# A hybrid DeltaNet and attention layer: later preparation steps, a gate by tanh, and one turn of the value blocks

## The chip, the cores and the metric

The kernel runs on one core of a Trainium2 chip. The metric is the device time of one execution in microseconds (us). The engines are TensorE (PE in the profile, its weight loads PEld), VectorE (DVE), ScalarE (ACT), GpSimd (POOL) and SyncE (SP), which issues most transfers. Each engine works through its own queue of instructions in order.

## The reference

One layer over 1024 latent tokens and 256 context tokens of width 1024. Cut to what matters here:

```python
px = modulate(rms_norm(x, norm1_w), sh1, sc1) @ w_in        # latent; pc the same for the context
qkv = short_conv(p[..., :3 * DN_WIDTH], conv_w)             # depthwise, 5 taps, then SiLU
a_mat = eye(CHUNK) + where(strict, (kb @ k^T) * decay, 0)   # CHUNK = 64, per head and direction
u = triangular_solve(a_mat, v * beta); w = triangular_solve(a_mat, kb * exp(gam))
# scan over chunks, forward and backward, the context first; then
o = rms_norm(o, out_norm_w) * silu(z)                       # gated DeltaNet, 4 heads of 128
na = neighborhood_attention(q, k, v, k_ctx, v_ctx, rpb)     # 8 heads of 64, window 8 x 16 + all context keys
x = x + g1 * (concatenate([o, na]) @ w_out)
x = x + g2 * swiglu(modulate(rms_norm(x, norm2_w), sh2, sc2), w_ffn_in, w_ffn_out)
```

## The kernel before

Every large product is made in fp32 precision out of three products of a high and a low part (`hh`, `hl` of the normed input, `whi`, `wlo` of the weights). Weights arrive as `wraw`; ScalarE casts the high part (L198, for wide jobs `zw` L584), and POOL subtracts to get the low part (L199, L585). For wide jobs `wraw` has one buffer, so the second half of a weight block is loaded when POOL has read the first.

The input projection is a list of jobs: a `Block` gives one head's 128 columns of k, q, v (DeltaNet) or nk, nq (attention) for all 1280 tokens, `Wide` jobs give 256 columns in tiles of 128 tokens (nv the attention's values, z the gate). Their order is k0 to k3, z1, nk0 to nk2, nv0, nk3, q0 to q3, nq0 to nq3, v0, nv1, v1, v2, v3, z0. A block's result lies in PSUM banks "blk" (four); ScalarE copies them to `cr` (L452) and so frees them; then come the convolution on VectorE (L456, L460), SiLU on ScalarE (L467), and transposes in `finish`.

Beside the jobs run background generators, a few steps for each group of products:

- `block_inverses` makes the 32 x 32 inverses that the scans need: tables of decay, a substitution on VectorE (L880, L882), then 32 transposes of `N` into `U` on TensorE (L892), four to a bank "m" (two banks), which ScalarE copies out (L894). The results go to `x_d`.
- `preps` makes, in ten steps of one pair of chunks each (forward and backward), the inverse y of a chunk's matrix: `rg` on POOL (L952), a product of `rg` and a constant (L964) for the decay `e`, a product `fx` by `kk` (L984) which ScalarE copies back to `kk` (L987), and then three blocks of y of 32, 64 and 96 columns (L995), each of which needs the copy of the one before (L997 on VectorE, L998 on ScalarE). The banks are "pr" (two). y is stored to `y_d` by SP (L1007). At most two steps are alive at once.

After v3 the job z0 runs beside the first tiles of the neighbourhood attention (scores L302, softmax L304 to L308, products with the values L323); then come the scans, the output projection and the feed-forward.

A scheduler puts each engine's instructions in order from the order in which they are written and from their estimated readiness; what it decides stands fast when the program is built. `keep_in_program_order` ties one instruction to its written place.

Of the kernel before, what the change touches and what calls it, by code (L numbers as in the profile page):

```python
# [9 lines left out]
F32 = mybir.dt.float32  # L10
# [3 lines left out]
AF = mybir.ActivationFunctionType  # L14
OP = mybir.AluOpType
# [73 lines left out]
def hybrid(ctx, tc, a, dbg):  # L89
# [56 lines left out]
    nv_d = dram.tile([T, 512], F32, name="nv_d", tag="nv_d")  # L146
    nq_d = dram.tile([NAH, 2, ND, L], F16, name="nq_d", tag="nq_d")
    nk_d = dram.tile([2, NAH, ND, T], F16, name="nk_d", tag="nk_d")
    vw_d = dram.tile([128, 4, 4, 4, 128], F32, name="vw_d", tag="vw_d")
    y_d = dram.tile([2, NCH, 128, 4, 128], F32, name="y_d", tag="y_d")  # L150
    at_d = dram.tile([2, 8, 128, 4, 128], F32, name="at_d", tag="at_d")
    x_d = dram.tile([128, 2, 2, NU, 32], F32, name="x_d", tag="x_d")
# [100 lines left out]
    def attention(nw):  # L253
# [20 lines left out]

        def values(hp, half, cb):
            vw = nw.tile([128, 3, 128], F32, name="vw", tag="vw", bufs=3)
            sp.dma_start(vw, vw_d[:, hp, cb, half:half + 3])
            return vw

        def context(hp):  # L280
# [93 lines left out]
    with ExitStack() as bs:  # L374
# [188 lines left out]
        class Wide:  # L563
# [32 lines left out]
            def tiles(self):  # L596
                half = self.half
                if self.kind == "nv":
                    for t in range(NCH):
                        p = self.wide(t, 0, 256)  # L600
                        vt = cp.tile([128, 272], F32, name="zt", tag="zt", bufs=2)
                        act.copy(vt[:, :256], p[:, :256])
                        act.dma_start(nv_d[t * 128:(t + 1) * 128, half * 256:half * 256 + 256], vt[:, :256])
                        yield
                    return
                if half == 1:
                    p = bank("blk")
                    for k in range(KT):
                        for j, (ww, x) in enumerate(((self.hi, hh), (self.hi, hl), (self.lo, hh))):
                            pe.matmul(p[:16, :CT], ww[:, k, 256:272], x[k][:, :CT], start=k == 0 and j == 0,  # L610
                                      stop=k == KT - 1 and j == 2)
                    abT = cp.tile([16, 272], F32, name="abT", tag="zt", bufs=2)
                    act.copy(abT[:, :CT], p[:16, :CT])
                    yield
                for t in range(2, NCH):
                    p = self.wide(t, 0, self.n)
                    if half == 0:
                        if t % 4 == 2:
                            zg = cp.tile([128, NCH, 128], F32, name="zg", tag="kx", bufs=3)
                            zg = zg.rearrange("p a b -> p (a b)")[:, :1024]  # L620
                        act.copy(zg[:, (t - 2) % 4 * 256:(t - 2) % 4 * 256 + 256], p[:, :256])
                        if t % 4 == 1:
                            act.activation(zg, zg, AF.Silu)
                            act.dma_start(z_d[(t - 5) * 128:(t - 1) * 128, 0:256].rearrange("(c p) d -> p c d", p=128),
                                          zg.rearrange("p (c d) -> p c d", d=256))
                        yield
                        continue
                    if t == 3:
                        q = bank()
                        for i in range(2):  # L630
                            pe.transpose(q[:, i * 16:i * 16 + 16], abT[:, i * 128:i * 128 + 128], ident[:16, :16])
                        act.copy(ab[:, 0:2].rearrange("p c d -> p (c d)"), q[:, :32])
                    zt = cp.tile([128, 272], F32, name="zt", tag="zt", bufs=2)
                    act.activation(zt[:, :256], p[:, :256], AF.Silu)
                    act.copy(ab[:, t], p[:, 256:272])
                    act.dma_start(z_d[(t - 2) * 128:(t - 1) * 128, 256:512], zt[:, :256])
                    yield
# [182 lines left out]
        def block_inverses():  # L820
            with ExitStack() as gs:
# [61 lines left out]
                    yield  # L883
                flat = N.rearrange("p b r c -> p b (r c)")
                dve.memset(flat[:P, :, 0:1024:33], 1.0)
                for _ in range(4):
                    yield
                U = WK.rearrange("p d u i -> p (d u) i")
                for i0 in range(0, 32, 4):
                    p = bank()  # L890
                    for i in range(4):
                        pe.transpose(p[:, i * P:(i + 1) * P], N[:P, :, :, i0 + i].rearrange("p b r -> p (b r)"),  # L892
                                     ident[:P, :P])
                    act.copy(U[:, :, i0:i0 + 4], p[:, :4 * P].rearrange("p (i u) -> p u i", i=4))  # L894
                    if i0 % 8 == 4:
                        yield
# [15 lines left out]
        def preps():  # L912

            first_half.close()
            with ExitStack() as gs:
# [28 lines left out]
                def prep(i, got):  # L944
# [10 lines left out]
                        for q in q32:  # L955
                            act.copy(fxs[d][q, :, q], xc[q, 1])
                    yield 1
                    if i == 0:
                        yield 1
                    es = []  # L960
                    for d, c, kk, xc, at in got:
                        p = bank("pr")
                        for j in range(2):
                            pe.matmul(p, mr[:, d], fl(rgs[2 * d + j]), start=j == 0, stop=False)  # L964
                        pe.matmul(p, mr[:, 4], mneg[:, d].rearrange("p (o i) -> p o i", o=1).to_broadcast(
                            [128, 4, 128]), start=False, stop=True)
                        e = work("e", 2)
# [18 lines left out]
                    for (d, c, kk, xc, at), p in zip(got, ps):  # L986
                        act.copy(fl(kk), p)  # L987
                    yield 1
                    for n in range(1, 4):
                        blk = (q32[3 - n], q32[n])  # L990
                        cols = (slice(128 - 32 * n, 128), slice(0, 32 * n))
# [8 lines left out]
                    for d, c, kk, xc, at in got:  # L1000
                        stores.append((y_d[d, c], y[d], tick[0] + 1))

                stores, tick = [], [0]

                def flush(n):
                    while stores and stores[0][2] <= n:
# [4 lines left out]
                while live or todo or landing:  # L1011
                    if not landing and todo and (todo[0] < 2 or all(x in done for x in queries)):
                        landing.append(fetch(todo.pop(0)))
                    if landing and (not live or len(live) < 2 and live[0][1] >= 4):
                        live.append([prep(*landing.pop(0)), 0])
                    if not live:
                        yield
                    for g in list(live):
# [30 lines left out]
        for n in range(2, len(jobs) + 2):  # L1049
# [21 lines left out]
            if isinstance(j, Wide):  # L1071
                for t, _ in enumerate(j.tiles()):
                    if t > 1 or not final:
                        next(fin, 0)
                    if final and t > 2:
                        next(fill)
                    if t == 4 and nrm:
# [16 lines left out]
            for _ in fin:  # L1094
                pass
            done.add(n - 2)
            if isinstance(j, Wide) and j.kind == "nv":
                hv = slice(2 * j.half, 2 * j.half + 2)
                vlat = nv_d[CT:].rearrange("(r c) d -> r c d", c=64)
                for cb in range(4):  # L1100
                    for ch in range(4):
                        for r in range(4):
                            rows = vlat[4 * ch + r, BLKS[cb]:BLKS[cb] + 32].rearrange("c (h d) -> c h d", d=128)
                            sp.dma_start(vw_d[r * 32:r * 32 + 32, hv, cb, ch], rows[:, hv])
            if nrm:
                nrm.norm()
            if isinstance(j, Block):
# [27 lines left out]
        dve.scalar_tensor_tensor(lo, p, onw, hi.bitcast(F32), op0=OP.mult, op1=OP.subtract)  # L1135

    with ExitStack() as gs:
        sl = pools(gs, "sl", "right", 3)
        shift(gs, "spad", "right", 16)
        sw = pools(gs, "sw", "right", 2)  # L1140
        gs.callback(scan_psum.close)
        ps = psum[-1]

# [12 lines left out]
        def load(d, c, near):  # L1156

            def tile_of(name, src):
                t = work(name, 3) if name == "v" else sl.tile([128, 4, 128], F32, name=name, tag=name)
                sp.dma_start(fl(t), src)  # L1160
                return t

# [189 lines left out]
    class Stream:  # L1352
# [67 lines left out]
        def next(self, n=2):  # L1420

            while len(self.got) < n:
                self.make()
            out = [self.got.pop(0) for _ in range(n)]
            return out
# [347 lines left out]
```

## Time and profile before

| | |
|---|---|
| time, median of 3 runs | 1541.6 us (1541.44 to 1543.45) |
| the profiled execution's own time | 1541.49 us |
| its span | 1539.4 us |
| TensorE busy | 1474.1 us, 96% |
| VectorE, ScalarE, POOL busy | 993.6, 728.2, 234.8 us |
| mean granted TensorE clock | 0.988 |
| moved by DMA | 267.36 MB, mean 174 GB/s |

The span is the time from the first instruction to the last; the execution's own time has some 2 us around it. Times in timeline rows are from the span's start: a row gives the start, the busy time, engine, line, operation, output<-input, how many instructions are grouped, and in brackets the idle time of the engine in front of them with what ended it. The granted clock is a share of full speed. "SPq" rows are the issuing of transfers by SP.

### The profile page before, as it was taken

The page shows a single profiled execution, that of the slowest core. Times are in us where ns is not written, and L with a number is a line of the kernel's source. Part 1 is how long each engine was busy: PE and PEld are TensorE (multiplying, and loading weights), DVE is VectorE, ACT ScalarE, POOL GpSimd, SP SyncE. Part 2 cuts the span into 40 slices and gives each one's busy share as a digit, 9 for nine tenths or more (in the row PEclk, how much of TensorE's full clock was granted, in tenths as well). Part 3 has the DMA queues.
Part 4 walks back from the last instruction along what each step waited for, and adds up shares of the span by engine and source line. Part 5 has one row for each costly group of instructions (what it writes and reads, how often), then busy time and mean ns, then how long its engine had stood idle before and what let it go on. Part 6 is the DMA issues. An engine that isn't in the chain of part 4 may idle for free. (4 is left out here: it accounts for less than half of the span.)

```text
span 1539.4 us, 24029 instructions
## 1 busy us (share of the span) xinstructions
PE 1474.1 (96%) x8702; PEld 1231.0 (80%) x8702; DVE 993.6 (65%) x1712; ACT 728.2 (47%) x1405; POOL 234.8 (15%) x286
## 2 busy tenths in 40 slices
PE   6999998899899898999999999999999999999999
PEld 3788797777688787788888878888888888888887
DVE  4774587974464354677977379855555566599652
ACT  5442552646764236666873176333333334354440
POOL 1054500634554100111210000000000000000000
PEclk9999999999999999999999999999999999999999
DMA  9274232687655557898638503533333334798742
GB/s 387 68 212 139 60 86 79 202 239 246 182 172 170 147 142 247 278 292 253 209 90 282 183 34 109 186 106 106 107 105 103 104 102 148 248 376 275 247 143 82
DMA packets 205142, 267.36 MB, mean 174 GB/s; under 512 B 17760, under 2 KB 115552, under 8 KB 204000
## 3 DMA queue, kind: packets, MB, share of 16 engines
q1 hardware_dynamic: 194320, 258.45, 52.4%
q10 hardware_dynamic: 10704, 7.38, 1.5%
q8 instruction: 68, 1.11, 0.3%
q14 instruction: 50, 0.41, 0.1%
HBM read 201.02 MB, written 68.94 MB: 175 GB/s over the span
## 5 line engine op out<-in xcount | busy, mean ns | idle before, releaser
L404 PE MATMUL blk<-hh,whi 128*128 128x512 f32 (+1 forms) x410 | 123.0, 394 | 6.8 <-ACT cr L452 5.3
L1410 ACT CAST uhi<-ws 128x512 fp32r<-128x512 f32 x91 | 54.0, 621 | 146.0 <-PE ps L1349 96.1
L1410 ACT CAST uhi<-wq 128x512 fp32r<-128x512 f32 x101 | 61.0, 622 | 130.9 <-issue 84.6
L404 PE MATMUL blk<-hl,whi 128*128 128x512 f32 (+1 forms) x410 | 115.4, 375 | 0.3 <-DVE hl L704 0.3
L404 PE MATMUL blk<-hh,wlo 128*128 128x512 f32 (+1 forms) x410 | 114.6, 375 | 0.6 <-POOL wlo L199 0.6
L592 PE MATMUL blk<-zw,hh 128*128 128x256 f32 (+1 forms) x576 | 113.5, 291 | 1.1 <-ACT cr L452 1.0
L1411 DVE TENSOR_TENSOR ulo<-wq,uhi 128x512 fp32r<-128x512 f32 x101 | 67.5, 687 | 58.4 <-ACT uhi L1410 32.4
L1349 PE MATMUL ps<-hT,uhi 128*128 128x512 f32 x336 | 103.6, 390 | 0.0
L1349 PE MATMUL ps<-lT,uhi 128*128 128x512 f32 x336 | 103.5, 389 | 0.0
L1349 PE MATMUL ps<-hT,ulo 128*128 128x512 f32 x336 | 103.4, 389 | 0.0
L592 PEld LDWEIGHTS blk<-zw,hh 128*128 128x128 f32 x576 | 91.7, 191 | 4.0 <-ACT cr L452 1.5
L1349 PE MATMUL ps<-hB,uhi 128*128 128x512 f32 x288 | 89.2, 391 | 0.6 <-ACT hB L1524 0.6
L1349 PE MATMUL ps<-lB,uhi 128*128 128x512 f32 x288 | 88.8, 389 | 0.4 <-DVE lB L1525 0.4
L1349 PE MATMUL ps<-hB,ulo 128*128 128x512 f32 x288 | 88.6, 389 | 0.0
L404 PEld LDWEIGHTS blk<-hh,whi 128*128 128x128 f32 x410 | 69.0, 194 | 21.9 <-ACT cr L452 6.1
L404 PEld LDWEIGHTS blk<-hl,whi 128*128 128x128 f32 x410 | 72.5, 192 | 14.9 <-DVE hl L704 0.8
L404 PEld LDWEIGHTS blk<-hh,wlo 128*128 128x128 f32 x410 | 72.5, 192 | 14.9 <-POOL wlo L199 0.9
L592 PE MATMUL blk<-zw,hl 128*128 128x256 f32 (+1 forms) x288 | 82.4, 286 | 0.0
L199 POOL TENSOR_TENSOR wlo<-wraw,whi 128x1024 fp32r<-128x1024 f32 x18 | 46.6, 2586 | 194.1 <-ACT whi L198 193.9
L1349 PEld LDWEIGHTS ps<-lT,uhi 128*128 128x128 f32 x336 | 63.1, 188 | 13.2
L1349 PEld LDWEIGHTS ps<-hT,ulo 128*128 128x128 f32 x336 | 63.1, 188 | 13.2
L1349 PEld LDWEIGHTS ps<-hT,uhi 128*128 128x128 f32 x336 | 62.9, 188 | 12.9
(362 smaller groups left out, 3526.1 us busy)
## 6 DMA issues: line engine op xcount, KB each, us to landing
wq<-w_fo SPq DMA_DIRECT2D x99, 256.0 KB, 4.1
wq<-w_gu SPq DMA_DIRECT2D x88, 256.0 KB, 2.9
wad<-wa SPq DMA_DIRECT2D x64, 256.0 KB, 4.2
bt<-rpb SPq DMA_DIRECT2D x64, 192.0 KB, 3.7
t_d<-g SPq DMA_DIRECT2D x22, 512.0 KB, 3.7
fr<-t_d SPq DMA_DIRECT2D x44, 256.0 KB, 5.2
f_d<-g SPq DMA_DIRECT2D x33, 256.0 KB, 2.1
fr<-f_d SPq DMA_DIRECT2D x33, 256.0 KB, 4.2
```

The source lines that it names most:

```text
L199: lo_engine.tensor_tensor(o, r, h.bitcast(F32), OP.subtract)
L404: pe.matmul(o, ww[:, k], xx[k][:, s], start=k == 0 and j == 0, stop=k == KT - 1 and j == 2)
L592: pe.matmul(p[:, :c1 - c0], x[k][:, s], ww[:, k, c0:c1], start=k == 0 and j == 0, stop=k == KT - 1 and j == 2)
L1349: pe.matmul(o, w[wi][:, k], x[xi][:, k], start=first and k == 0 and j == 0, stop=k == n - 1 and j == 2, skip_group_check=True)
L1410: act.copy(hi, self.raw[key])
L1411: dve.tensor_tensor(lo, self.raw[key], hi.bitcast(F32), OP.subtract)
```

## The change

Six things are edited.

1. The last four tiles of z0 compute z * sigmoid(z) as (tanh(z/2) + 1) * z/2: ScalarE makes tanh and a halved copy, VectorE adds and multiplies. The SiLU over these four tiles goes. The tiles' buffer is now `cr`, the convolution's.
2. The window values are stored to `vw_d` in a layout of whole rows of 512, by 16 transfers of 256 KB after nv1. Before there were 64 transfers of 32 KB after each of nv0 and nv1.
3. The first of each four transposes of `N` is kept in program order, and six empty steps stand before them where four stood.
4. The first preparation step begins ten ticks later, with its rg products kept in program order; every preparation step has one more empty step between the copy of `kk` and the first y block.
5. In z0, what is left of v3's `finish` is issued after tile 4.
6. The scans' loaded tiles, v among them, lie over the convolution's buffers, and their work tiles where these lay.

```diff
-    vw_d = dram.tile([128, 4, 4, 4, 128], F32, name="vw_d", tag="vw_d")
+    vw_d = dram.tile([128, 4, 4, 512], F32, name="vw_d", tag="vw_d")
...
-            sp.dma_start(vw, vw_d[:, hp, cb, half:half + 3])
+            sp.dma_start(vw, vw_d[:, cb, half:half + 3, hp * 128:hp * 128 + 128])
...
-                            zg = cp.tile([128, NCH, 128], F32, name="zg", tag="kx", bufs=3)
-                            zg = zg.rearrange("p a b -> p (a b)")[:, :1024]
-                        act.copy(zg[:, (t - 2) % 4 * 256:(t - 2) % 4 * 256 + 256], p[:, :256])
+                            zg = cp.tile([128, T], F32, name="zg", tag="cr", bufs=2)
+                            zg = zg[:, :1024]
+                        zc = zg[:, (t - 2) % 4 * 256:(t - 2) % 4 * 256 + 256]
+                        if t < 6:
+                            act.copy(zc, p[:, :256])
+                        else:
+                            th = cp.tile([128, 272], F32, name="zt", tag="zt", bufs=2)
+                            act.activation(th[:, :256], p[:, :256], AF.Tanh, scale=0.5)
+                            act.activation(zc, p[:, :256], AF.Copy, scale=0.5)
+                            dve.scalar_tensor_tensor(zc, th[:, :256], 1.0, zc, op0=OP.add, op1=OP.mult)
                         if t % 4 == 1:
-                            act.activation(zg, zg, AF.Silu)
+                            if t == 5:
+                                act.activation(zg, zg, AF.Silu)
...
-                for _ in range(4):
+                for _ in range(6):
                     yield
...
-                        pe.transpose(p[:, i * P:(i + 1) * P], N[:P, :, :, i0 + i].rearrange("p b r -> p (b r)"),
-                                     ident[:P, :P])
+                        t = pe.transpose(p[:, i * P:(i + 1) * P], N[:P, :, :, i0 + i].rearrange("p b r -> p (b r)"),
+                                         ident[:P, :P])
+                        if not i:
+                            tc.keep_in_program_order(t)
...
-                    if i == 0:
+                    for _ in range(LATE if i == 0 else 0):
                         yield 1
...
-                            pe.matmul(p, mr[:, d], fl(rgs[2 * d + j]), start=j == 0, stop=False)
+                            m = pe.matmul(p, mr[:, d], fl(rgs[2 * d + j]), start=j == 0, stop=False)
+                            if i == 0:
+                                tc.keep_in_program_order(m)
...
                         act.copy(fl(kk), p)
                     yield 1
+                    yield 1
                     for n in range(1, 4):
...
-                stores, tick = [], [0]
+                LATE, stores, tick = 10, [], [0]
...
-                        live.append([prep(*landing.pop(0)), 0])
+                        live.append([prep(*landing.pop(0)), 0 if live or len(todo) < NCH - 1 else -LATE])
...
+                    if final and t > 4:
+                        for _ in fin:
+                            pass
...
-            if isinstance(j, Wide) and j.kind == "nv":
-                hv = slice(2 * j.half, 2 * j.half + 2)
-                vlat = nv_d[CT:].rearrange("(r c) d -> r c d", c=64)
+            if isinstance(j, Wide) and n == values:
+                vlat = nv_d[CT:].rearrange("(n r c) d -> r c n d", r=4, c=64)
                 for cb in range(4):
-                    for ch in range(4):
-                        for r in range(4):
-                            rows = vlat[4 * ch + r, BLKS[cb]:BLKS[cb] + 32].rearrange("c (h d) -> c h d", d=128)
-                            sp.dma_start(vw_d[r * 32:r * 32 + 32, hv, cb, ch], rows[:, hv])
+                    for r in range(4):
+                        sp.dma_start(vw_d[r * 32:r * 32 + 32, cb], vlat[r, BLKS[cb]:BLKS[cb] + 32])
...
+        sw = pools(gs, "sw", "right", 2)
+        shift(gs, "spad", "right", 16)
         sl = pools(gs, "sl", "right", 3)
-        shift(gs, "spad", "right", 16)
-        sw = pools(gs, "sw", "right", 2)
...
-                t = work(name, 3) if name == "v" else sl.tile([128, 4, 128], F32, name=name, tag=name)
+                t = sl.tile([128, 4, 128], F32, name=name, tag=name)
```

The scheduler's answer shows at three places. The first is TensorE in nq3, at a preparation step that begins with the products of `fx` and `kk`; the y block of 32 columns follows. Before:

```order
L984 MATMUL pr<-fx_2513,kk 128x128 x3
L984 MATMUL pr<-fx_2514,kk 128x128 [waits DVE_49]
L984 MATMUL pr<-fx_2514,kk 128x128 x3
L404 MATMUL blk<-hh_130,whi 128x512 x2
L404 MATMUL blk<-hl_131,whi 128x512 x2
L404 MATMUL blk<-hh_130,wlo 128x512 x2
L995 MATMUL pr<-y_2517,kk 32x32 [waits Activation_49]
```

And now, at the same place:

```order
L996 MATMUL pr<-fx_2462,kk 128x128 [waits Activation_49]
L996 MATMUL pr<-fx_2462,kk 128x128 x3
L404 MATMUL blk<-hh_130,whi 128x512 x2
L404 MATMUL blk<-hl_131,whi 128x512 x2
L404 MATMUL blk<-hh_130,wlo 128x512 x2
L404 MATMUL blk<-hh_132,whi 128x512 x2
L404 MATMUL blk<-hl_133,whi 128x512 x2
L404 MATMUL blk<-hh_132,wlo 128x512 x2
L404 MATMUL blk<-hh_134,whi 128x512 x2
L404 MATMUL blk<-hl_135,whi 128x512 x2
L404 MATMUL blk<-hh_134,wlo 128x512 x2
L1008 MATMUL pr<-y_2465,kk 32x32 [waits Activation_49]
```

Six products of the job stood between; now there are eighteen.

The second place is ScalarE at the end of the input projection: `cr` copies of v2 and v3, SiLU of v1, v2 and v3, and the casts of z0's weights `zw`. Before:

```order
L584 CAST zw<-wraw 128x8x128 [waits DMAHW0_49]
L467 ACT_TABLE_LOAD
L467 ACTIVATE cacc<-cacc 128x1280 [waits DVE_49]
L452 COPY cr<-blk 128x256 [waits PE_49]
L452 COPY cr<-blk 128x512 [waits PE_49] x2
L467 ACTIVATE cacc<-cacc 128x1280 [waits DVE_49]
L584 CAST zw<-wraw 128x8x128 [waits DMAHW7_49]
L534 DMA v_d<-vt 128x10x128 [waits DMAHW0_49,DVE_49]
L452 COPY cr<-blk 128x256 [waits PE_49,Activation_49]
L452 COPY cr<-blk 128x512 [waits PE_49] x2
```

Now, from v3's copies on:

```order
L452 COPY cr<-blk 128x256 [waits PE_49,Activation_49]
L452 COPY cr<-blk 128x512 [waits PE_49] x2
L1011 COPY y_2466<-pr 32x4x32 [waits DMAHW2_49,PE_49]
L1011 COPY y_2466<-pr 32x4x64 [waits PE_49]
L467 ACTIVATE cacc<-cacc 128x1280 [waits DVE_49,Activation_49]
L1011 COPY y_2466<-pr 32x4x96 [waits PE_49]
L584 CAST zw<-wraw 128x8x128 [waits DMAHW7_49]
L584 CAST zw<-wraw 128x8x128 [waits DMAHW2_49]
L623 COPY zg<-blk 128x256 [waits DVE_49,PE_49,Activation_49]
```

Both casts moved from in front of v2's and v3's copies to behind v3's SiLU, and the last preparation's copies of y stand between. On TensorE that preparation's blocks (L1008) stand between v3's last product and z0's first.

The third place is SP, where z0's weights are loaded. Before, both halves stood behind the stores of all y, the second after the attention's first loads:

```order
L1007 DMA y_d<-y_2517 128x512 [waits DMAHW6_49,DVE_49,Pool_49]
L1007 DMA y_d<-y_2518 128x512 [waits DMAHW7_49,Activation_49,Pool_49]
L583 DMA wraw<-w_z 128x8x128 [waits DMAHW0_49,Pool_49]
L259 DMA qs<-nq_d 128x1024 [waits DMAHW1_49,PE_49]
L261 DMA kh<-nk_d 64x1280 [waits DMAHW2_49,PE_49]
```

Now:

```order
L583 DMA wraw<-w_z 128x8x128 [waits DMAHW7_49,Pool_49]
L1020 DMA y_d<-y_2465 128x512 [waits DMAHW0_49,DVE_49,Pool_49]
L1020 DMA y_d<-y_2466 128x512 [waits DMAHW1_49,Activation_49,Pool_49]
L583 DMA wraw<-w_z 128x8x128 [waits DMAHW7_49,DMAHW2_49,Pool_49]
L259 DMA qs<-nq_d 128x1024 [waits DMAHW3_49,PE_49]
L261 DMA kh<-nk_d 64x1280 [waits DMAHW4_49,PE_49]
```

The last two stores of y moved between the two halves, and all of the attention's loads behind the second.

## The prediction

> **What bounds the kernel now.** I read the page first, then busy time by stage, then the half-clock stretches, then the timeline of TensorE with the waits in front of each instruction.
>
> ```profile
> span 1539.4 us, 24029 instructions
> PE 1474.1 (96%) x8702; PEld 1231.0 (80%) x8702; DVE 993.6 (65%) x1712; ACT 728.2 (47%) x1405; POOL 234.8 (15%) x286
> ```
>
> TensorE is busy for 96% of the span: 65 us of idle time in all, so an edit pays by taking TensorE's waits away, or by sparing it half clock. The windows by stage (length, PE busy, granted clock) say where they lie:
>
> ```profile
> 245.00:310.00 65.00, 55.11 (x269) 0.89 0.49 152
> 310.00:530.00 220.00, 210.41 (x1507) 0.98 0.62 189
> 530.00:560.00 30.00, 24.46 (x140) 0.89 0.81 209
> 560.00:640.00 80.00, 69.70 (x625) 1.00 0.69 219
> 805.00:1539.40 734.40, 728.69 (x3228) 1.00 0.48 160
> ```
>
> The last 734 us (output projection and feed-forward) wait for 6 us and are not touched by the edit: I cost them at nothing. The edit acts between 245 and 640. There the clock drops too:
>
> ```profile
> 255.84:262.66 6.82, 4.17 (x16) 0.50 0.19 50
> 293.38:300.21 6.83, 5.83 (x17) 0.50 1.01 315
> 399.20:402.61 3.41, 3.41 (x10) 0.50 0.49 111
> 443.57:446.98 3.41, 3.41 (x21) 0.50 0.77 223
> 532.32:539.14 6.82, 4.63 (x13) 0.50 1.07 255
> 440.16:443.57 3.41, 1.34 (x17) 1.00 0.05 12
> ```
>
> Each of the first five rows is one or two windows of 3.41 us at clock 0.50; half of its busy time is lost. The last row is the window ahead of 443.57: TensorE did not stop for a whole window, it worked 1.34 us of 3.41, and the next window ran at half. So on this kernel two waits of 2 us close together already cost a further 1.7 us.
>
> The waits themselves (timeline rows and, for three lines, the groups between 245 and 560; the last bracket or column is the idle time and its releaser):
>
> ```profile
> 258.17 0.53 PE L892 MATMUL m<-cst,N 80*128 80x80 f32 x2 [5.66 <-DVE N L885]
> L964 PE MATMUL pr<-rg,mr 128*128 128x512 f32 x40 | 14.2, 428 | 2.7 <-POOL rg L952 2.7
> L984 PE MATMUL pr<-fx,kk 128*128 128x128 f32 x160 | 20.3, 277 | 1.6 <-DVE kk L971 1.1 <-DVE y L997 0.5
> L995 PE MATMUL pr<-y,kk 128*32 128x32 f32 (+2 forms) x480 | 26.1, 224 | 7.3 <-ACT kk L987 7.3
> 397.24 0.25 PE L995 MATMUL pr<-y,kk 128*32 128x32 f32 x2 [2.01 <-ACT kk L987]
> 534.51 0.80 PE L404 MATMUL blk<-hh,whi 128*128 128x512 f32 x1 [5.32 <-ACT cr L452]
> 552.94 0.38 PE L592 MATMUL blk<-zw,hh 128*128 128x256 f32 x1 [1.03 <-ACT cr L452]
> ```
>
> **The change part by part.** Six terms, minus is a gain.
>
> *(1) Transposes of the inverses.* In TensorE's order they now stand two groups of six matmuls later in q0. Six matmuls take 1.36 us, from the starts of two groups:
>
> ```profile
> 249.62 0.62 PE L404 MATMUL blk<-hh,whi 128*128 128x512 f32 x2
> 250.98 0.61 PE L404 MATMUL blk<-hh,whi 128*128 128x512 f32 x2
> 272.51 1.05 ACT L492 ACTIVATE cr<-m,bias 128x256 f32<-128x256 f32 x2
> ```
>
> So 2.7 of the 5.66 us are covered and 2.9 stay. Half clock cost 4.17/2 = 2.1; I take one window, 1.7, for what stays. But the last eight transposes now come behind q1's norm sums and only six matmuls, and want the two "m" banks which ScalarE empties after a table load (1.28, row in part 6) and the two activations of the last row (1.05): 2.3 against 1.36 us of cover and the queue ahead, 1 to 2.4, I take 2. Now 5.66 + 2.1 = 7.8; then 2.9 + 1.7 + 2.0 = 6.6: **-1.2** (-3 to +0.5).
>
> A rule speaks here. The Trainium skill, "TensorE: Matmul & The Clock Gate", section "HAM oscillation — how this bites in real kernels", has it that only idle gaps over about 3.4 us throttle. By it the 2.9 us that stay cost no half clock and the sum would be 1.7 us lower, 1534.5; the window at 440.16 above contradicts it, so I go by the window.
>
> *(2) The first preparation step, ten ticks later.* Its four rg matmuls waited 2.7 us for POOL, the fx product 1.1 for VectorE, and the stretch 293.38 to 300.21 at half clock cost 5.83/2 = 2.9: 6.7 in all. Between the four rg matmuls now stand matmuls of q2 only in part, and POOL makes the same tables; I leave 0.7: **-6.0** (-6.7 to -3).
>
> *(3) One empty step before the y blocks, in all ten preparations.* L995 waited 7.3 us for ScalarE's copy of kk. At the 397.24 wait six matmuls stood between the fx product and the first y block; now 18 do, so 2.7 us of cover come on top and the 2.01 are hidden. The two windows from 399.20 and 443.57 go with them, 1.7 each: 10.7 in all. Some of it will come back as waits of the 32-64-96 chain, which nothing lengthens; I leave 1.5: **-9.2** (-10.7 to 0; nothing is gained if the next copy is late instead).
>
> *(4) The values' turn in 16 transfers.*
>
> ```profile
> 530.57 1.05 ACT L584 CAST zw<-wraw 128x1024 fp32r<-128x1024 f32 x1 [13.89 <-DMA wraw<-w_z]
> 514.49 7.42 SPq L1104 DMA_DIRECT2D vw_d<-nv_d  x11
> ```
>
> SP needs 0.67 us for each of these transfers and had 64 of them in front of z0's weights. ScalarE's cast waited for the weights 13.89 us, and the copies that free v2's banks stood behind the cast: that is the 5.32 at 534.51. Now there are 16, and no cast stands in front of those copies. What is left is a bank wait like the 1.03 at 552.94: 4.3 gained, and 4.63/2 = 2.3 of half clock: **-6.6** (-6.6 to -4.3).
>
> *(5) What the later preparations push out: a new wait ahead of z0.* Steps that start ten ticks later and have one tick more end later. In the new order the last preparation's three y blocks stand behind all of v3 on TensorE; on VectorE its copies of y lie between v3's convolution products, on ScalarE behind v3's SiLU; both casts of z0's weights stand behind these; and on SP the second half of the weights stands behind the two stores of that y and waits until POOL has read the first half (one raw buffer). Before, both casts were done by 544.6. The new chain, in rows:
>
> ```profile
> 551.54 1.35 ACT L452 COPY cr<-blk 128x256 f32<-128x256 f32 x3 [6.93 <-PE blk L404]
> 553.92 5.90 DVE L460 SCALAR_TENSOR_TENSOR cacc<-cr,cw,cacc 128x255 f32<-128x255 f32 x6
> L997 DVE COPY y<-pr 32x128 f32<-32x128 f32 (+2 forms) x30 | 12.5, 417 | 35.6 <-PE pr L995 35.1
> 559.86 1.28 ACT L467 ACTIVATE cacc<-cacc 128x1280 f32<-128x1280 f32 x1 [0.55 <-DVE cacc L460]
> L998 ACT COPY y<-pr 32x128 f32<-32x128 f32 (+2 forms) x30 | 10.9, 365 | 31.7 <-PE pr L995 28.1 <-DVE y L997 3.4
> 543.58 1.03 ACT L584 CAST zw<-wraw 128x1024 fp32r<-128x1024 f32 x1
> 544.69 2.40 POOL L585 TENSOR_TENSOR zw<-wraw,zw 128x1024 fp32r<-128x1024 f32 x1 [10.64 <-ACT zw L584]
> wraw<-w_z SPq DMA_DIRECT2D x2, 544.0 KB, 3.9
> wraw<-w_z SPq DMA_DIRECT2D x2, 512.0 KB, 5.4
> 565.58 0.27 PE L302 MATMUL sc<-kh,qs 128*128 128x256 f16 x1
> ```
>
> In the time of before: v3's products end at 553.92 + 5.90 = 559.8, with three copies of 0.42 in between 561.1; SiLU 1.28, the last copy 0.37, the first cast 1.03: 563.8; POOL's low part 2.40: 566.2; the second half issued and landed, 3.9 to 5.4: 570.1 to 571.6; its cast 1.03: 571.1 to 572.6. z0 started at 552.94, so 18.2 to 19.7 later, 18.9. After four matmuls it needs the second low part (2.40 of POOL, about 1 us covered at half clock): +1.4. So long a pause brings half clock, as the pauses at 258 and 534 did with 2.1 and 2.3: +2.4. The 48 small matmuls that stand here no longer stand earlier, a tenth of 26.1 us: at most -2.6, I take -2. Sum **+20.7** (+17 to +25). The attention's own loads stand behind the second half on SP too. Their first use came 12.6 us after z0's start (565.58); five issues and a landing fit into that. Were that cover gone, each us of lateness would be a us more; that is in the upper end.
>
> *(6) tanh for the last gate group, buffers of the scans.* Between 584 and 592 ScalarE loads two tables and runs one SiLU for z0, and TensorE waits for ScalarE's pt and VectorE's bt:
>
> ```profile
> 584.02 1.28 ACT L623 ACT_TABLE_LOAD   x1
> 585.32 1.06 ACT L623 ACTIVATE zg<-zg 128x1024 f32<-128x1024 f32 x1
> 588.52 1.28 ACT L306 ACT_TABLE_LOAD   x1
> 588.55 0.32 PE L323 MATMUL sc<-pt,vc 128*64 128x128 f32 x1 [0.78 <-ACT pt L316]
> 591.66 0.74 PE L313 MATMUL sc<-cst,bt 128*128 128x128 f32 x5 [1.80 <-DVE bt L308]
> ```
>
> 3.6 us leave ScalarE; four tanh of about 0.37 come, spread over z0's last four tiles. Of the waits I count 2.6 (0.78 + 1.80) and 0.4 for the scans' loads, whose buffers come free with the convolution: **-3.0** (-5 to +1). By the Trainium skill, "ScalarE: Activation LUTs", section "What ACT_TABLE_LOAD costs", a switch costs about 2.66 us with its drain, so 1.4 us more each; here the SiLU starts 1.30 after the load did, which shows no drain, and I go by that.
>
> Sum: -1.2 - 6.0 - 9.2 - 6.6 + 20.7 - 3.0 = -5.3. The profiled execution's own time is 1541.49 (span 1539.4), the median 1541.6: 1541.5 - 5.3 = **1536.2 us**.
>
> **The rivals.**
>
> *Slower: the chain of the y blocks stays as late as it was, and the wait ahead of z0 remains.* For it: 7.3 us of waits are put down to one copy on ScalarE, and a preparation's blocks depend on one another through copies on two engines, so a later start can meet the next copy late. Against it: 2.7 us of new cover beat the single wait shown, 2.01. Then term 3 is worth nothing and the sum is +3.9: 1545.4; with term 5 at its upper end, 1549.7. It decides once less than 3.9 of term 3's 9.2 comes through. Chance 0.30.
>
> *The wait ahead of z0 does not come.* If the last preparation were through before v3 ended, term 5 would be about -2 to +3 and the time about 1515. The order speaks against it: no engine passes its own queue. Chance 0.05.
>
> *It all cancels.* Term 5 at 24, or terms 2 and 3 a third smaller: 1541. Chance 0.10.
>
> **How the numbers follow.** The forecast, faster at about 1536, has 0.55. 0.2% (3.1 us) is about what a measurement of this kernel can tell from no change. Faster: 0.55 + 0.05 = 0.60; same 0.10; slower 0.30. The range takes the forecast's own bounds down to 1527 (term 5 at 17, terms 1 and 6 at their better ends) and reaches up to the slower case, 1550; the 1515 case is left out.
>
> **What would show it.** Right: no wait of over 1 us at L1008 between 310 and 530, no half clock at 293 and 399, under 1.5 us ahead of v3, and one pause of 17 to 22 us ahead of z0's first matmul, released by ScalarE's cast, with half clock behind it. Wrong: z0 starting within 5 us of v3's end; waits at the y blocks of the old size; or waits of over 5 us in all behind z0 for qs, kh or bt, which would mean that the attention's loads had lost their cover.

## The result and the profile after

| | before | changed |
|---|---|---|
| median | 1541.32 us (14 runs) | 1545.22 us (14 runs) |
| profiled execution, own time | 1541.49 us | 1544.3 us |
| span | 1539.4 us | 1542.2 us |

The ratio is 1.0032, 95% interval 1.002 to 1.0044: slower by 3.9 us between the medians (3 to 7 by the interval), where the forecast was 5.3 us faster. That is the time that the slower rival gave (+3.9). It is inside the range, with the wrong sign. Traces here and below are each of one execution, whose own time can lie up to 5 us from the median of its kernel: what an edit is worth goes by medians, while waits, order and the lengths of stretches are read from traces.

The page of the changed kernel, then the windows by stage (length, PE busy, granted clock, share of DMA, GB/s):

```profile
span 1542.2 us, 23924 instructions
PE 1470.6 (95%) x8702; PEld 1231.2 (80%) x8702; DVE 988.7 (64%) x1716; ACT 726.1 (47%) x1405; POOL 237.4 (15%) x286
```

```profile
245.00:310.00 65.00, 58.76 (x277) 0.89 0.53 166
310.00:530.00 220.00, 207.68 (x1482) 0.99 0.59 185
530.00:560.00 30.00, 13.16 (x96) 0.68 0.44 125
560.00:640.00 80.00, 74.93 (x647) 0.95 0.84 259
295.00:305.90 10.90, 10.07 (x36) 0.53 0.87 275
```

From 310 to 530 the clock rose only from 0.98 to 0.99, and TensorE waited 12.3 us, 2.7 more than before. From 530 to 560 it was busy 13.16 us of 30, where it had been 24.46. The last row is a stretch inside the first, at mean clock 0.53; the half clock itself lasted from 295.00 to 305.24, longer than either stretch of before in that stage.

Lost time can be counted as idle time plus half of what was busy at clock 0.5. Between 245 and 530 it was 27.9 us before (19.5 idle, 16.8 busy at half clock) and is 26.7 us now (18.6 and 16.2); the forecast for this part (terms 1 to 3) was -16.4. Between 530 and 640 it rose from 18.2 to 28.8 us.

What TensorE waits for between 245 and 530, by groups (busy, mean ns, then idle time and its releasers):

```profile
L1008 PE MATMUL pr<-y,kk 128*32 128x32 f32 (+2 forms) x432 | 22.1, 223 | 9.5 <-ACT e L980 3.4 <-DVE y L1010 3.3 <-ACT kk L999 2.1
L996 PE MATMUL pr<-fx,kk 128*128 128x128 f32 x160 | 20.4, 278 | 1.8 <-ACT y L1011 1.6 <-DVE kk L983 0.2
L974 PE MATMUL pr<-rg,mr 128*128 128x512 f32 x40 | 13.8, 422 | 1.2 <-ACT y L1011 0.6 <-DVE y L1010 0.6
L485 PE MATMUL m<-ones,cr 128*128 128x1 f32 x64 | 9.2, 273 | 3.1 <-ACT cr L470 3.1
L900 PE MATMUL m<-cst,N 80*128 80x80 f32 x32 | 4.9, 294 | 2.9 <-DVE N L893 2.1 <-ACT cr L492 0.5 <-DVE N L890 0.4
```

The wait for the copy of kk fell from 7.3 to 2.1, the wait of rg on POOL is gone, and the transposes wait 2.9 instead of 6.0. Against the removed waits stand new ones: 3.4 behind ScalarE's `e`, 3.3 and more behind the copies of y, and 3.1 in q1's norm sums (L485), which waited 0.2 before.

The timeline of TensorE around v3 and z0. The first row belongs to the start of v3, the second is v3's last product; the same product started at 551.16 before. Before, v3 began with the idle 5.32:

```profile
522.35 0.39 PE L404 MATMUL blk<-hh,whi 128*128 128x512 f32 x1
536.24 0.75 PE L404 MATMUL blk<-hh,wlo 128*128 128x256 f32 x3
542.63 1.49 PE L1008 MATMUL pr<-y,kk 128*32 128x64 f32 x16 [5.12 <-DVE y L1010]
544.58 1.49 PE L1008 MATMUL pr<-y,kk 128*32 128x96 f32 x16 [0.45 <-ACT y L1011]
556.12 0.58 PE L592 MATMUL blk<-zw,hh 128*128 128x256 f32 x1 [10.05 <-ACT zw L584]
558.56 0.79 PE L592 MATMUL blk<-zw,hh 128*128 128x256 f32 x2 [1.21 <-POOL zw L585]
```

At the end of v3 the changed kernel leads by 551.16 - 536.24 = 14.9 us. Half of it, 7.5, is the wait ahead of v3 that went. z0 then starts at 556.12 against 552.94: the lead is spent, and 3.2 us more. z0 itself loses about another 4.8 us to half clock and its second weight half, and the scans give back 4.9 of that.

The chain ahead of z0, on ScalarE, POOL and SP. The waits of SP (last three rows; total, times, longest) are those from 500 to 556:

```profile
545.75 1.27 ACT L467 ACTIVATE cacc<-cacc 128x1280 f32<-128x1280 f32 x1 [1.23 <-DVE cacc L460]
547.54 1.04 ACT L584 CAST zw<-wraw 128x1024 fp32r<-128x1024 f32 x1
548.72 2.34 POOL L585 TENSOR_TENSOR zw<-wraw,zw 128x1024 fp32r<-128x1024 f32 x1 [36.71 <-ACT zw L584]
555.02 1.04 ACT L584 CAST zw<-wraw 128x1024 fp32r<-128x1024 f32 x1 [6.44 <-DMA wraw<-w_z]
533.96 0.38 ACTq L534 DMA_DIRECT2D v_d<-vt  x1
537.68 0.61 SPq L583 DMA_DIRECT2D wraw<-w_z  x1
551.08 0.60 SPq L583 DMA_DIRECT2D wraw<-w_z  x1
SPq L583 <- DMA v_d<-vt: 28.6, 1, 28.6
SPq L1020 <- DVE y L1010: 15.7, 3, 8.4
```

ScalarE casts the first half behind v3's SiLU, POOL reads it, SP issues the second half at 551.08, it lands at 555.0, is cast, and z0 starts at 556.12: link by link the chain of term 5. So of the prediction's signs of being right, those of terms 4 and 5 came: no wait ahead of v3, and a pause of some 19 us from v3's end (the y blocks within it) to z0's first product. Those of terms 2 and 3 did not: L1008 waits 3.38 us in one place, and the half clock stands from 295 as it stood from 293. What the prediction did not have is the SP row of 28.6 us. SP reached the first half's load at about 509 and stood there until ScalarE's store of one head's values, issued at 533.96, had landed (3.7 us). The two have no data in common. In the changed kernel's order the load waits for DMAHW7 (quoted ahead of the prediction). It is one of eight completion semaphores, which the program's transfers take in turn (the transfers quoted there wait for DMAHW7, 0, 1, 2, 3, 4), and the transfer that has it before is that store, on ScalarE's queue:

```
L534 DMA v_d<-vt 128x10x128 [waits DMAHW7_49,DVE_49]
```

### The profile page after: what moved, and what is told of

Same layout as the page of the kernel before. It is cut to its first block, busy times and chain, and to the rows that moved or that the text cites. A ratio compares the mean times of both kernels' runs of the same rounds, so it can differ in the third digit from the quotient of the medians.

```text
span 1542.2 us, 23924 instructions
## 1 busy us (share of the span) xinstructions
PE 1470.6 (95%) x8702; PEld 1231.2 (80%) x8702; DVE 988.7 (64%) x1716; ACT 726.1 (47%) x1405; POOL 237.4 (15%) x286
## 5 line engine op out<-in xcount | busy, mean ns | idle before, releaser
L592 PEld LDWEIGHTS blk<-zw,hh 128*128 128x128 f32 x576 | 93.6, 194 | 16.4 <-ACT zw L584 10.4
```

The costliest lines, as they stand in the source:

```text
L592: pe.matmul(p[:, :c1 - c0], x[k][:, s], ww[:, k, c0:c1], start=k == 0 and j == 0, stop=k == KT - 1 and j == 2)
```

## Experiments

The changed kernel has three groups of edits that can be told apart: the turn of the value blocks (term 4), the late first preparation with tied rg and the empty step (terms 2 and 3), and the rest (terms 1 and 6). My theory after the result: the turn makes the pause ahead of z0, since it changes what SP waits for and where the casts stand. The rival is the prediction's own account: the later preparations make it.

**The turn alone**, put into the kernel before:

```diff
-            if isinstance(j, Wide) and j.kind == "nv":
+            if isinstance(j, Wide) and n == values:
+                vlat = nv_d[CT:].rearrange("(n r c) d -> r c n d", r=4, c=64)
...
+                        sp.dma_start(vw_d[r * 32:r * 32 + 32, cb], vlat[r, BLKS[cb]:BLKS[cb] + 32])
```

> The kernel before with the turn of the value blocks alone (16 transfers after nv1). Theory of the late y blocks: the wait ahead of z0 came from the last preparation's y blocks, which stay early here, so no pause over 2 us ahead of z0; the 5.3 us wait at v2 to v3 and its half clock go, about -7 us: 1534. Rival, the weights' transfer: the turn itself makes z0's first weights late. In the trace of the changed kernel SP waited 28.6 us with that transfer for a store of v1's values (v_d); if the transfers and the store count on one of the eight completion semaphores, the order of 16 transfers brings them together and the wait is there without any late y block: a pause of 8 to 15 us at z0 and no gain, 1540 to 1548.

It took 1552.43 us, ratio 1.0072 (1.0052 to 1.0091): the turn by itself costs some 11 us, more than either expectation. TensorE's timeline and SP's longest wait:

```profile
552.78 0.59 PE L302 MATMUL sc<-kh,qs 128*128 128x256 f16 x2 [8.06 <-DMA kh<-nk_d]
559.27 0.37 PE L302 MATMUL sc<-kh,qs 128*128 128x256 f16 x1 [3.94 <-DVE mx L304]
562.27 0.66 PE L313 MATMUL sc<-cst,bt 128*128 128x128 f32 x2 [1.77 <-DVE bt L308]
SPq L583 <- DMA v_d<-vt: 32.6, 1, 32.6
```

The wait ahead of v3 is gone here too, with 7.5 us, as term 4 said. But SP stands 32.6 us for the same store, z0's weights are issued at 545.42 (525.45 before), and the attention's first loads, queued behind them, with them. In this order the attention's scores come ahead of z0 and are late. No preparation is later than before, so the rival does not explain this pause.

**The changed kernel without the empty step** (`yield 1` after the copy of kk taken out):

> The changed kernel without the empty step ahead of the y blocks; the first preparation stays ten ticks late. The y blocks of the last preparation then stand ahead of v3's. Late y blocks: the pause ahead of z0 goes (under 3 us), about -18 us, and the waits at the y blocks between 310 and 530 grow by at most 3: 1528 to 1532. The weights' transfer: the pause shrinks to 8 to 15 us, because SP still issues z0's weights after v1's store; 1538 to 1544. The waits at the y blocks tell what the step was worth by itself: 7 us more of them if my term was right, no more than 2 if the chain of copies was late for another reason.

1542.74 us, 1.0012 (1.0000 to 1.0023), inside what was expected if the weights' transfer makes the pause. Against the changed kernel's 1545.22 that is 2.5 us less, with intervals that overlap by a hair: the empty step, which the forecast had save 9.2 us, saves nothing that can be told and may cost. Without it the y blocks wait for kk again and for little else between 245 and 530, and the pause ahead of z0 takes the form that the turn alone gave it:

```profile
L1007 PE MATMUL pr<-y,kk 128*32 128x32 f32 (+2 forms) x480 | 25.9, 224 | 8.7 <-ACT kk L999 8.7
548.67 0.59 PE L302 MATMUL sc<-kh,qs 128*128 128x256 f16 x2 [7.86 <-DMA kh<-nk_d]
SPq L583 <- DMA v_d<-vt: 32.6, 1, 32.6
```

8.7 us of waits behind one producer against 9.5 spread over three; in the changed kernel 48 more of these products stand behind v3 and wait another 5.6.

**The changed kernel without the late first preparation**, rg still tied:

```diff
-                    for _ in range(LATE if i == 0 else 0):
+                    for _ in range(1 if i == 0 else 0):
...
-                        live.append([prep(*landing.pop(0)), 0 if live or len(todo) < NCH - 1 else -LATE])
+                        live.append([prep(*landing.pop(0)), 0])
```

> The changed kernel with the first preparation step where it was (one empty tick), its rg products still kept in program order. If the later start was worth 6 us: the waits for rg (2.7) and kk (1.1) and the half clock from 293 come back, about +6: 1551. If the later start only exchanged waits (the 3.1 us at q1's norm sums and three half-clock windows behind it, 295 to 306, in the changed kernel): within 2 us of 1545. The pause ahead of z0 stays under both, since the last y blocks still stand behind v3.

1547.84 us, 1.004 (1.0026 to 1.0055); the interval overlaps the changed kernel's, and the time lies between the two expectations. No wait of rg on POOL came back, so the late start is not what removed it, and the 3.1 us in q1's norm sums stayed:

```profile
297.27 2.26 PE L485 MATMUL m<-ones,cr 128*128 128x1 f32 x16 [3.13 <-ACT cr L470]
556.46 0.58 PE L592 MATMUL blk<-zw,hh 128*128 128x256 f32 x1 [10.67 <-ACT zw L584]
```

**Breaking the shared semaphore.** One of the turn's 16 transfers is cut in two, which moves every later SP transfer to the next semaphore in turn. Once in the changed kernel, once in the turn alone:

```diff
-                        sp.dma_start(vw_d[r * 32:r * 32 + 32, cb], vlat[r, BLKS[cb]:BLKS[cb] + 32])
+                        for a0, a1 in ((0, 2), (2, 4)) if cb * 4 + r < 1 else ((0, 4),):
+                            sp.dma_start(vw_d[r * 32:r * 32 + 32, cb, a0:a1], vlat[r, BLKS[cb]:BLKS[cb] + 32, a0:a1])
```

> The changed kernel with one of the 16 transfers cut into two, so that each later transfer counts on the next completion semaphore; nothing else is edited, the last y blocks still stand behind v3. The weights' transfer: SP issues z0's first weights near 510 instead of 537.7, the pause ahead of z0 gets shorter by 3 us or more (first cast before v3's SiLU). Late y blocks: the pause stays at 17 to 20 us, since it is made of v3's convolution, the y copies and the second half of the weights behind the y stores; time within 3 us of 1545.

> The kernel before with the turn alone and one of its transfers cut in two, nothing else. The order is that of the turn alone but for the place of the first cast (ahead of v3's SiLU, not behind it), and z0's first weights count on another completion semaphore than v1's store. If the shared semaphore held SP for 32.6 us and with it the attention's loads, SP issues the weights before 520 and the attention's loads soon after, the 8.1 us wait for kh behind v3 goes, and the time falls by 6 to 12 us from 1552. If it was the amount of data or the size of a transfer, wait and time stay.

1548.81 us (1.0052, 1.0035 to 1.0069) and 1550.24 us (1.0058, 1.0037 to 1.008): no gain that can be told in either, and neither the shorter pause of the first expectation nor the 6 to 12 us of the second. z0's first weights did go out early, at 512.87 and 517.73. SP's longest waits, first of the one, then of the other:

```profile
SPq L1020 <- DVE y L1010: 41.5, 2, 35.2
```

```profile
SPq L259 <- DMA v_d<-vt: 26.6, 1, 26.6
```

In the first, SP now stands 35 us at the stores of the last y, with the attention's loads behind them. In the second the attention's first load has inherited the semaphore. So the hold on one load is real, but removing it alone gains nothing: what comes next in SP's queue is late as well. For the same reason these two runs don't rule out that the size of the transfers counts.

**Loads moved forward**: six of the turn's transfers cut in two and z0's weights fetched one job earlier, in the turn alone and in the changed kernel:

```diff
-            if n + 1 < len(jobs):
+            if n + 1 < len(jobs) - 1:
...
+            if n == len(jobs) - 3:
+                jobs[n + 2].prefetch()
```

> The kernel before with the turn of the value blocks alone, six of its 16 transfers cut in two (22), and z0's weights asked for one job earlier. In the order the first cast of z0's weights now stands ahead of v3's copies and the second right behind them. If the turn alone was slow (1552) because z0's first weights waited for v1's store on a shared completion semaphore and everything behind them on SP with it, SP issues them before 520, TensorE's pauses between v3 and z0 fall from 13.8 to under 5 us and the 7 us of the v2 to v3 term show: 1532 to 1538. If large transfers are slow by themselves, the time stays over 1545 although the semaphore differs.

> The changed kernel with the same two edits (22 transfers, z0's weights one job earlier); late start, empty step, tanh and tied transposes stay. In the order the last y blocks now stand ahead of v3's last products and the casts around v3's copies. If the pause ahead of z0 (10 us for the cast, 5 for the y blocks, half clock behind them) was the price of the order that the turn made, it falls under 4 us and the time to 1522 to 1530. If the late preparations make it by themselves, whatever the transfers do, a pause of over 10 us stays and the time is over 1538.

The turn alone came to 1544.90 us (1.0034, 1.0015 to 1.0052) from 1.0072, the changed kernel to 1540.42 (0.9989, 0.9975 to 1.0003) from 1.0032. Both edits together take back part of the loss, so these loads' lateness is part of it; but neither kernel reached its expectation (1532 to 1538 and 1522 to 1530). In the changed kernel z0 still waits 8.79 us for the second cast:

```profile
552.17 0.58 PE L592 MATMUL blk<-zw,hh 128*128 128x256 f32 x1 [8.79 <-ACT zw L584]
540.79 1.05 ACT L584 CAST zw<-wraw 128x1024 fp32r<-128x1024 f32 x1 [0.74 <-DVE vt L530]
551.07 1.04 ACT L584 CAST zw<-wraw 128x1024 fp32r<-128x1024 f32 x1 [6.72 <-DMA wraw<-w_z]
```

The last y blocks now lie within v3, and both casts ahead of v3's SiLU. But the first half of the weights, issued at 510.44, is cast only at 540.79: on ScalarE that cast stands behind the last copies of y and the store of one head's values. So SP could issue the second half only at 544.38. In the turn alone with its loads moved forward, where no preparation is late, the first cast stands behind that store too, at 539.42.

**The changed kernel with the turn undone**, all else kept, and **with the late start, the tied rg and the empty step taken out too**:

> The changed kernel with the turn undone alone: 64 small transfers after each of nv0 and nv1. If the turn makes the pause ahead of z0, SP no longer waits near 30 us for v1's store, the last y blocks stand ahead of v3's end, and the pause falls to under 9 us (the second cast still stands behind the attention's first exponentials): 1535 to 1542, with the wait at v2 to v3 back or not as the casts stand. If the late start and the empty step make it, the pause stays at 15 us or more and the time at 1545 or above.

> The changed kernel without the turn, the late start, the tie of the rg products and the empty step: tied transposes, tanh, the scans' buffers and z0's early finish remain, so the small transfers and the 5.3 us wait at v2 to v3 come back. My terms for what remains: -1.2 and -3.0, 1537. The checkpoints of the changed trace say -3.2 and -4.9: 1533. No gain at all (1541) if the gain behind z0 in the changed kernel was only lateness caught up.

1537.07 us (0.9969, 0.9955 to 0.9983) and 1537.49 us (0.9967, 0.9955 to 0.998), both as expected. TensorE around v3 and z0 in the first:

```profile
540.57 0.50 PE L404 MATMUL blk<-hh,whi 128*128 128x512 f32 x1 [2.37 <-ACT cr L452]
557.48 0.39 PE L592 MATMUL blk<-zw,hh 128*128 128x256 f32 x1 [1.03 <-ACT cr L452]
```

The late start and the empty step stand in this kernel as in the changed one, and there is no pause ahead of z0: 1.03 us, as before. That decides against term 5's cause: late preparations make no such pause without the turn. The two kernels differ by 0.4 us: terms 2 and 3 together are worth nothing that can be told here (the intervals leave some 3 us either way, not 15). Undoing the turn is worth 1545.22 - 1537.07 = 8.2 us.

**The values turned in 32 half transfers**, 16 of 128 KB after each of nv0 and nv1, in the same layout; in the kernel before, then with the rest (terms 1 and 6), then with the late start and tied rg as well, without the empty step:

```diff
             if isinstance(j, Wide) and j.kind == "nv":
+                hv = slice(256 * j.half, 256 * j.half + 256)
...
+                        sp.dma_start(vw_d[r * 32:r * 32 + 32, cb, :, hv], vlat[r, BLKS[cb]:BLKS[cb] + 32, :, hv])
```

> The kernel before with 16 transfers of 128 KB after each of nv0 and nv1 (32 in all), nothing else. In the order the first cast of z0's weights stands ahead of v2's copies, behind v1's SiLU, and the second ahead of v3's copies, as before the change; z0 comes right behind v3. The gain that I forecast for the turn, 6.6 us (5.3 of wait at v2 to v3 and its half clock), should show here if few transfers are what it takes and the order is not spoilt: 1534 to 1537. If the wait at v2 to v3 stays over 4 us, the small transfers were not its cause.

> The 32 larger transfers with the tied transposes, tanh and the scans' buffers; no late start, no empty step. Sum of the two runs' gains if they add up: 4 from those parts (1537.5) and 4 to 6.6 from the transfers: 1531 to 1534. If they don't add up, 1537 or more.

> The same with the late first preparation and its tied rg products, still without the empty step. The changed kernel was 2.6 us faster than its version without the late start, an uncertain difference: if the late start is worth that, 1529 to 1532; if it only exchanges waits, as halves_rest within 1.5 us.

1531.85 us (0.9945, 0.9924 to 0.9966), 1529.17 us (0.9919, 0.9896 to 0.9941) and 1525.47 us (0.9894, 0.9874 to 0.9913). Each beats what was expected of it, and all three beat both the kernel before and the changed one. The first, from 530 to 560 and at z0, with the casts:

```profile
530.00:560.00 30.00, 28.95 (x202) 1.00 0.51 140
544.50 0.38 PE L592 MATMUL blk<-zw,hh 128*128 128x256 f32 x1 [1.03 <-ACT cr L452]
526.79 1.03 ACT L584 CAST zw<-wraw 128x1024 fp32r<-128x1024 f32 x1
SPq L259 <- DMA v_d<-vt: 7.9, 1, 7.9
```

Here is term 4's gain as it was meant: fewer transfers in front of z0's weights (issued at 516.94), no wait ahead of v3, the first cast done at 527.8, and no pause. The store of v still holds SP, but for 7.9 us and at a load that has time. The last two differ by 3.7 us, the late start and tied rg, with intervals that overlap. That has the sign of the 2.6 us by which the changed kernel beat its version without the late start. The empty step measured 2.5 us the other way. So the 0.4 us of terms 2 and 3 may be a small gain and a small cost that cancel; no run puts either clear of noise.

## Why the prediction was wrong

Sums by groups, from the medians above:

| terms | forecast | measured | from |
|---|---|---|---|
| 1 and 6 | -4.2 | -4.0 | the rest alone against before, 1537.49 - 1541.45 |
| 2 and 3 | -15.2 | -0.4 | turn undone against the rest alone, 1537.07 - 1537.49 |
| 4 and 5 | +14.1 | +8.2 | changed against turn undone |
| sum | -5.3 | +3.8 | measured directly: +3.9 |

The three rows share their kernels, so their sum meets the direct figure by construction; it is no check. The two wrong groups erred in opposite directions. Had I had terms 2 and 3 right and nothing else, I would have forecast 1551; that the slower rival's time was met so closely is in part luck, two errors that cancel.

- **Term 3 is the step that failed**, with term 2: not the cover ("2.7 us of cover come on top and the 2.01 are hidden"), for the wait for kk did shrink, to 2.1, but the 1.5 us left for what would come back as other waits (0.7 in term 2). The two terms stood at -15.2 and measured -0.4. The row counted one producer of a chain; with later blocks TensorE waited for others, the copies of y and `e`. For `e` the rows show why: on ScalarE it stood behind a cast whose weights had not landed. What made the copies of y late is not shown. The rows of ScalarE and TensorE there:

```profile
404.36 1.04 ACT L584 CAST zw<-wraw 128x1024 fp32r<-128x1024 f32 x1 [5.60 <-DMA wraw<-w_nv]
405.43 1.09 ACT L980 ACTIVATE e<-pr 128x512 f32<-128x512 f32 x2
406.08 1.34 PE L1008 MATMUL pr<-y,kk 128*32 128x96 f32 x16 [3.38 <-ACT e L980]
```

  The rival, at 0.30, had this mechanism right; the cause that it gave for the pause ahead of z0 was wrong, as in the forecast.
- **Term 2**: rg's wait on POOL went, but it is gone in the rest alone too, which has neither the late start nor the tie. What came is the 3.1 us at q1's norm sums, with 10.2 us at half clock behind it. It also comes in the rest alone (3.1), so I book both on term 1; the moved transposes are the only edit of that kernel at this place, but no run has them alone. VectorE around q1's convolution, in the changed kernel:

```profile
285.82 2.60 DVE L460 SCALAR_TENSOR_TENSOR cacc<-cr,cw,cacc 128x1022 f32<-128x1022 f32 x2
288.33 1.50 DVE L910 STREAM_TRANSPOSE ut<-WK 128x1280 f32<-128x1280 f32 x1
289.76 1.24 DVE L460 SCALAR_TENSOR_TENSOR cacc<-cr,cw,cacc 128x1023 f32<-128x1023 f32 x1
290.92 1.48 DVE L913 TENSOR_TENSOR WK<-WK,NB 128x1280 f32<-128x1280 f32 x1
292.33 1.28 DVE L460 SCALAR_TENSOR_TENSOR cacc<-cr,cw,cacc 128x1022 f32<-128x1022 f32 x1
295.83 3.57 PE L485 MATMUL m<-ones,cr 128*128 128x1 f32 x16 [3.13 <-ACT cr L470]
```

  The table transpose and its product, 1.50 + 1.48 us, now stand within this convolution, and the wait behind it is 3.13. In the kernel before, the last of them was over 8 us ahead of q1's convolution:

```profile
284.06 1.48 DVE L903 TENSOR_TENSOR WK<-WK,NB 128x1280 f32<-128x1280 f32 x1
293.71 1.45 DVE L456 TENSOR_SCALAR cacc<-cr,cw 128x1024 f32<-128x1024 f32 x1
```

- **Term 1**: the transposes wait 3.1 us less, and that new wait is their price. **Term 6**: -4.9 in the changed kernel's own trace (from z0's last product to the output projection), -5.1 in that of the rest alone, -3.0 forecast.
- **Term 4** had its mechanism right where it looked, ahead of v3 (-7.5 against -6.6), and its sign wrong. I priced the transfers that go, and did not follow the load they had stood in front of: for what it would wait next, and where the casts would go. The order that I quoted showed it, "waits DMAHW7_49"; I read the line and not whose transfer had that semaphore before.
- **Term 5** was near in size at z0's end (+22.9 against +20.7, between the ends of v3 and z0) and wrong in cause: the empty step only decides whether y blocks or the attention's scores stand in the pause. It should have been booked on term 4.
- Two sums in the prediction's working don't come out, without weight for the result: with term 5 at 24 the time is 1539.5, not 1541, and the named bounds give a lower end of 1528.7, not 1527. And the window at 440.16 held one wait, not two.

Open: why the scheduler sets the casts behind v3's SiLU with the 16 large transfers and not with 32 half ones. And whether the half transfers win by their size, their earlier place or the semaphores that they happen to get: no run separates these.

## What to carry to other kernels

When an edit takes away what stood in front of a load, follow the load: read in the new order what it waits for now, down to which older transfer shares its semaphore, and book the cost to that edit. A wait on one link of a chain is worth what remains when the next link is late, not its own length. Splitting a batch of transfers in moderate pieces placed as early as their data allow beat 64 small ones after each half by some 9 us here, and one late block by some 20.

## What the runs showed of the hardware

In these traces a single wait of 2 us can be followed by half clock, and its price is not fixed. The window at 440.16 in the prediction held a single wait, of 2.07 us, and 3.41 us at clock 0.50 followed. The wait of 3.1 us at q1's norm sums is in seven traces, at the same place and with the same releaser. The half clock that followed lasted 10.24 us in three of them (the changed kernel, the turn undone, the rest alone), 6.83 in two (without the empty step, without the late start) and 3.41 in two (one transfer cut in two, loads moved forward in the changed kernel). The longest, then one of the shortest (columns as in the windows by stage):

```profile
295.00:305.24 10.24, 9.41 (x30) 0.50 0.85 271
302.62:306.03 3.41, 3.41 (x9) 0.50 0.97 314
```

So the same wait cost 1.7 to 4.7 us beyond itself, half of the busy time in the row, and a difference of this size between two traces shows no effect of an edit. In the three long cases the half clock began 0.7 to 0.8 us ahead of the sixteen 128x1 products that end the wait, in the others 1.4 to 2.1 us behind their start; whether such products count as work for the clock, no run shows. Nor does the length of a wait decide: two waits of 0.65 and 1.20 us, at 412.49 and 413.91 in the last of the half-transfer kernels, were followed by 3.41 us at half clock; the same two in the kernel before, at 419.00 and 420.41, by none, and 2.58 us at 526.22 with the turn undone by none either. The Trainium skill, "TensorE: Matmul & The Clock Gate", section "HAM oscillation — how this bites in real kernels", lets only gaps over about 3.4 us throttle: all waits named here were shorter, so the window at 440.16 was no exception to the measurements.

SP stood for 28.6 us (changed kernel), 32.6 (the turn alone) and 26.6 (the turn alone with one transfer cut in two) at a load that needed no data from the store it waited for. The Trainium skill, "DMA: Bandwidth & Descriptors", section "Anatomy of one DMA — SWDGE (gpsimd) path", has every semaphore wait happen on the issuing sequencer ahead of dispatch; these rows agree, and all loads queued behind were late with it.
